# A decoder layer on Trainium2: identity transposes ahead of the first rows, a new order of row scaling and loads, and one product of the second FFN issued earlier

## The chip, the cores and the metric

The kernel runs on one core of one Trainium2 chip. The metric is the time of one execution on the device in microseconds (us), as the median of several runs; lower is better. Engines are named as in the profile: PE is TensorE (matmuls), PEld its weight loads, DVE is VectorE, ACT is ScalarE, POOL is GpSimd, and SP is SyncE, which issues most of the DMAs.

## The reference, cut to what matters

One layer works on 1,024 tokens of width 1,024, ahead of which 16 learned meta tokens stand, all in float32:

```
h = h + 1/2 * SwiGLU_1(RMSNorm(h))            # first FFN,  D_FF = 2816
u = RMSNorm(h) @ W_in
o = concat[ HGRN2(u_hgrn), StickBreaking(u_sb) ]
h = h + o @ W_out
h = h + 1/2 * SwiGLU_2(RMSNorm(h))            # second FFN
SwiGLU(h):  g, u = split(h @ w_in);  (silu(g) * u) @ w_out
RMSNorm(x): x * rsqrt(mean(x*x) + 1e-6) * gain
```

The change touches two places: the first microseconds of the first FFN (its norm, and the turning of x so that the width lies on partitions) and the first products of the second FFN's `w_in`.

## The kernel before, in words

**Products.** Each float32 operand is kept as a rounded part (hi, type float32r) and a remainder (lo), and a product is three matmuls per block of 128: hi by hi, lo by hi, hi by lo (`times`, L448). ACT makes the hi part and DVE subtracts for the lo part: for weights in `operand` (L358, the rows L360 and L362), for tokens in `first` (L834, the rows L837 and L838) or in `halve` (L304, the rows L309 and L310).

**The FFN's first matrix.** `fast_in` (L350) multiplies 2 by 2 blocks by a fast scheme with seven products: B11, B21, T2, T3, T1, T4, B22, each one of 12 matmuls (4 blocks by 3) into the PSUM banks qa, qb and qc. A `quad` is a generator that issues the products of one column; a `pair` is two quads, one for the gate and one for the up half. The first pairs are `opened`: their products are issued in an order written out by hand, a `next(...)` at a time, because the operands are still being made. In the first FFN there are four opened pairs, with the order in `open_tokens` (L792); in the second FFN there are two, and after their B11 and B21 products `in_turns` (L585) takes turns between gate and up. An opened quad of the second FFN has a step that only fetches the next weights (`ready.append(next(w))`, L498) ahead of its T2 product (L500). Before the change line 601 steps `opened[0]`, the first gate, over that fetch, and not `opened[1]`, its up half. So in the turns the gate issues T2 while the up half fetches, then the gate issues T3 and the up half T2.

**Operands of the second FFN.** B11 and B21 come from the first 512 tokens, the T operands also from the second 512 tokens. `blocks_b` (L321) makes them bit by bit: each `next(feed)` makes the next group, and T3's group (L341 to L343) is requested when the first T3 product is about to be issued (L465 and L466).

**The first rows.** `open_tokens` loads four tiles of 128 rows of x (`ra`, L840, `rows_in` at L809, 512 KB each, on SP's queue). Each row is squared and summed (`row_sum`, L759: ACT's Square with an accumulator, or a DVE operation), its root taken on ACT and inverted on DVE (`row_root`, L768), and the tile scaled on DVE (`row_scale`, L774). PE then turns 128 by 128 blocks against the identity (`turned`, L780) into PSUM, six of the eight blocks of each row tile first. `first` multiplies by the norm's gain g1 and splits. The second four tiles (`rb`, L852) are summed, scaled and turned later, in a list of items (L924 to L933) that interleaves with the opened products.

**What sets the order.** PE's order is that of the program everywhere. In `open_tokens` the orders of ACT, DVE and SP are those of the program too (L1904); elsewhere a scheduler at build time places the instructions of these engines. Instructions of one engine run in order.

**The gain.** g1 is a 4 KB vector that is spread over 128 partitions in pieces of 4 bytes. It is loaded by a DMA that ACT issues (L104), before anything else. `ng1`, its negative, is made on DVE at L1826 and is used in `combine` (L881).

Of the kernel before, what the change touches and what calls it, by code (L numbers as in the profile page):

```python
# [11 lines left out]
F32 = mybir.dt.float32  # L12
# [8 lines left out]
P = 128  # L21
D = 1024
KT = D // P
SEQ = 1024
META = 16
# [23 lines left out]
class Block:  # L49
# [19 lines left out]
    def setup(self):  # L69
        nc, a = self.nc, self.a  # L70
        self.loads = []
        self.const = c = self.pool("const")
        c.tile([P, 368], F32, name="base")
        self.pool("edge", side="right").tile([P, 504], F32, name="edge")
        self.dram = self.pool("scratch", space=DRAM)

        self.ident = c.tile([P, P], F32, name="ident")
        nc.vector.memset(self.ident, 1.0)
        nc.gpsimd.affine_select(
            out=self.ident, in_=self.ident, pattern=[[-1, P]],  # L80
            compare_op=ALU.is_equal, fill=0.0, base=0, channel_multiplier=1,
        )
        self.ones_d = c.tile([P, P], F32, name="ones_d")
        nc.vector.memset(self.ones_d, 1.0 / D)
        self.eps = c.tile([P, 1], F32, name="eps")
        nc.vector.memset(self.eps, EPS)
        nc.scalar.activation(c.tile([P, 1], F32, name="root"), self.eps, AF.Sqrt)

        self.g1 = self.column(a["ffn1_norm"][0], KT, "g1")
        self.gm = self.column(a["mix_norm"][0], KT, "gm")  # L90
        self.g2 = self.column(a["ffn2_norm"][0], KT, "g2")
        self.og = self.column(a["hgrn_out_norm"][0], 4, "og")
        self.l0 = self.column(a["hgrn_lb_logits"][0], 4, "l0")
        self.l1 = self.column(a["hgrn_lb_logits"][1], 4, "l1")
        self.qg, self.kg, self.qg8 = (c.tile([P, 1], F32, name=x) for x in ("qg", "kg", "qg8"))
        for h in range(2):
            s = slice(64 * h, 64 * h + 64)
            self.loads.append((self.qg[s], a["sb_q_norm"].rearrange("a d -> d a")))
            self.loads.append((self.kg[s], a["sb_k_norm"].rearrange("a d -> d a")))
        self.mx, self.lb, self.lbc = (c.tile([P, 4], F32, name=x) for x in ("mx", "lb", "lbc"))  # L100
        self.masks = c.tile([P, len(LEVELS), P], U8, name="masks")
        self.ss = c.tile([P, 9, 2], F32, name="ss_x")
        self.ng1 = c.tile([P, KT], F32, name="ng1")
        nc.scalar.dma_start(*self.loads.pop(0))  # L104

    def setup_rest(self):

# [242 lines left out]
    def fast_in(self, ops, n, w_in, actD, openers, ev0, open_ev, feed=None, meta=None, spare=None,  # L350
                between=lambda: None, after_opened=lambda: None, late=lambda: None, taken=lambda at, step=True: None):

        nc = self.nc
# [240 lines left out]
        opened = [q for f in range(0, 2 * openers, 2) for q in pair(f, "first")]  # L594
        if feed:
            for i in range(0, 2 * openers, 2):
                for _ in range(2):
                    for q in opened[i : i + 2]:
                        next(q)
                        yield  # L600
            next(opened[0])
            next(feed)
            made_yet.add("T2")
        else:
            yield opened, prepare
# [186 lines left out]
    def open_tokens(self, ops, opened, prepare, rows_at, ev, operands):  # L792
# [9 lines left out]
        nc, x = self.nc, self.a["x"][0]  # L802
        stt, sub = nc.vector.scalar_tensor_tensor, nc.vector.tensor_sub
        g = [self.g1[:, k : k + 1] for k in range(KT)]
        rp = self.pool("rows", ctx=rows_at, side="right")
        junk = [rp.tile([P, D], (BF16, U8)[i], name=f"junk{i}") for i in range(2)]
        order = [q for i in range(0, len(opened), 2) for _ in range(2) for q in opened[i : i + 2]]

        def rows_in(r0):  # L809
            got = []  # L810
            for i in range(4):
                row = rp.tile([P, D], F32, tag="row", name="row", bufs=8)
                nc.sync.dma_start(row, x[r0 + i * P : r0 + i * P + P])
                got.append(row)
            return got
# [14 lines left out]
        def spare(*ks):  # L830
            for k in ks:
                nc.scalar.mul((b11 + b21)[k], kept[k], g[k])

        def first(*ks):  # L834
            for k in ks:
                hi, lo = (t[:, k % 4, :] for t in ops[("B11", "B21")[k // 4]])
                nc.scalar.mul(hi, kept[k], g[k])  # L837
                stt(lo, kept[k], g[k], hi.bitcast(F32), ALU.mult, ALU.subtract)  # L838

        ra = rows_in(0)  # L840
        self.masks_blank(sd)
        for i in range(3):
            self.row_sum(ra[i], i, junk, nc.vector if i == 1 else nc.scalar)
            self.row_root(ra[i], i)
        for i in range(3):
            self.row_scale(ra[i], i)
        self.row_sum(ra[3], 3, junk, nc.scalar)
        self.row_root(ra[3], 3)
        self.row_scale(ra[3], 3, 2)
        next(order[0])  # L850
        next(order[1])
        rb = rows_in(512)  # L852
        meta = rp.tile([META, D], F32, name="meta")
        kept.update(self.turned(ra, range(6), "bbccdd"))
        first(0, 1, 2, 3)
        nc.vector.tensor_scalar_mul(b11[0], kept[0], g[0])
        spare(1)
        next(order[2])
        nc.sync.dma_start(meta, self.a["meta_tokens"])
        first(4, 5)  # L860
        self.row_sum(rb[0], 4, junk, nc.vector)
        next(order[0])
        next(order[1])
        kept.update(self.turned(ra, (6, 7), "bb"))
        first(6, 7)
        next(order[3])

        def turn_b22():
# [907 lines left out]
    def run(self):  # L1776
        nc, tc, a = self.nc, self.tc, self.a
# [20 lines left out]
        with ExitStack() as c0:  # L1798
            with ExitStack() as c1:
# [8 lines left out]
                with tc.manual_schedule(engines={nc.tensor.engine}), ExitStack() as c2:  # L1808
# [14 lines left out]
                    operands(xa, ("B11", "B21"))  # L1823
                    self.pin = self.pool("pin1", 1, PSUM, c2)
                    self.t_bufs, self.in_bufs = 2, 10
                    nc.vector.tensor_scalar_mul(self.ng1, self.g1, -1.0)  # L1826

                    def ahead_of_time(pool):

# [73 lines left out]
                    opened, prepare = next(steps)  # L1903
# [266 lines left out]
                with tc.manual_schedule(engines={nc.tensor.engine}):  # L2170
# [7 lines left out]
                    with ExitStack() as c2:  # L2178
                        self.att.append(self.pool("att1", ctx=c2))
                        tag = self.proj_tags[0]  # L2180
# [214 lines left out]
```

## Time and profile before

| | |
|---|---|
| runs | 1955.10, 1956.52, 1956.65 us; median 1956.52 |
| the profiled execution's own time | 1955.73 us |
| its span, first to last instruction | 1953.8 us |
| PE busy | 1918.7 us (98%) |
| DVE busy | 1394.1 us (71%) |
| ACT busy | 849.2 us (43%) |

The profile is one execution. Times in its views count from the start of the span. The timeline merges neighbouring instructions of one kind on one engine: start, duration of the group, engine, line, operation, output and inputs, shapes and count; in brackets stands the idle time of the engine ahead of it and what ended that. A row with SPq or ACTq is the issue of a DMA and not its transfer.

### The profile page before, as it was taken

What the parts mean: (1) busy time and instruction counts of PE and PEld (TensorE: products, weight loads), DVE (VectorE), ACT (ScalarE), POOL (GpSimd) and SP (SyncE); (2) the same over time, 40 slices, a digit from 0 to 9 for tenths busy, and PEclk for the clock granted to TensorE, in tenths of its full rate; (3) what the DMA queues carried; (4) which work ended last, traced back from release to release, by engine and by line L of the source; (5) the groups of instructions that cost most, each with busy time, mean ns of one, the idle gap of its engine ahead of it and who ended that gap; (6) DMA issues with size and microseconds to landing.
All of it is one profiled execution on the core that took longest, in us unless ns stands there. A gap on an engine that the chain in (4) does not pass through costs nothing.

```text
span 1953.8 us, 30198 instructions
## 1 busy us (share of the span) xinstructions
PE 1918.7 (98%) x10607; PEld 1616.5 (83%) x10607; DVE 1394.1 (71%) x2184; ACT 849.2 (43%) x1711; POOL 451.2 (23%) x625
## 2 busy tenths in 40 slices
PE   7999999999999999999999999999999999999999
PEld 6888888887888888888898978887888888888887
DVE  6977778877678665467777766667567767766774
ACT  6523343334444544356666635533233332344443
POOL 3010100001000003133333332210544644530000
PEclk9999999999999999999999999999999999999999
DMA  7356888757976315865453178655544444469473
GB/s 212 93 158 177 249 278 256 233 193 282 373 235 189 126 55 143 192 172 148 134 153 115 57 252 242 151 207 185 193 118 135 131 129 125 129 244 323 150 232 113
DMA packets 381687, 355.54 MB, mean 182 GB/s; under 512 B 129040, under 2 KB 284560, under 8 KB 381536
## 3 DMA queue, kind: packets, MB, share of 16 engines
q1 hardware_dynamic: 359728, 288.98, 49.0%
q0 software_dynamic: 20768, 64.63, 9.6%
q8 instruction: 84, 1.38, 0.3%
q14 instruction: 67, 0.55, 0.1%
q10 hardware_dynamic: 1040, 0.00, 0.0%
HBM read 237.95 MB, written 115.57 MB: 181 GB/s over the span
## 4 chain that ended last, share of the span: by engine, by line
PE 91%; DVE 5%; ACT 2%; issue 1%; POOL 1%; DMA 1%; SPq 0%; DVEq 0%; ACTq 0%; POOLq 0%
PE o L734 21%; PE qb L452 18%; PE qc L452 12%; PE qa L452 12%; PE proj L249 5%; PE proj L251 5%; PE proj L250 5%; PE flip L1497 2%; PE wo L249 1%; PE wo L251 1%; PE wo L250 1%; PE mq L1003 1%; PE oacc L1574 1%; PE oacc L1572 1%; PE z L1642 1%
## 5 line engine op out<-in xcount | busy, mean ns | idle before, releaser
L452 PE MATMUL qb<-T,wh 128*128 128x512 f32 x1056 | 344.6, 390 | 1.6 <-ACT T L309 0.8
L452 PEld LDWEIGHTS qb<-T,wh 128*128 128x128 f32 x1056 | 198.1, 188 | 47.0 <-issue 3.2
L452 PE MATMUL qa<-B,wh 128*128 128x512 f32 x696 | 227.7, 392 | 0.0
L362 DVE TENSOR_TENSOR wl<-s,wh 128x512 fp32r<-128x512 f32 x160 | 166.0, 1037 | 68.8 <-ACT wh L360 67.8
L249 PE MATMUL proj<-xh,wh 128*128 128x512 f32 (+2 forms) x640 | 212.4, 332 | 2.6 <-ACT st L1144 1.3
L734 PE MATMUL o<-t,w 128*128 128x512 f32 x924 | 212.1, 390 | 1.0 <-DVE u L545 0.9
L251 PE MATMUL proj<-xl,wh 128*128 128x512 f32 (+2 forms) x640 | 209.8, 328 | 0.8 <-DVE xl L1959 0.8
L250 PE MATMUL proj<-xh,wl 128*128 128x512 f32 (+2 forms) x640 | 209.7, 328 | 0.0
L734 PE MATMUL o<-parts 128*128 128x512 f32 x924 | 209.6, 389 | 0.0
L452 PE MATMUL qb<-T,wl 128*128 128x512 f32 x528 | 205.5, 389 | 0.0
L734 PEld LDWEIGHTS o<-t,w 128*128 128x128 f32 x924 | 172.7, 188 | 38.4 <-ACT sgm L983 1.2
L734 PEld LDWEIGHTS o<-parts 128*128 128x128 f32 x924 | 173.4, 188 | 36.0
L360 ACT CAST wh<-s 128x512 fp32r<-128x512 f32 x160 | 99.5, 623 | 185.2 <-PE qb L452 140.4
L452 PEld LDWEIGHTS qa<-B,wh 128*128 128x128 f32 x696 | 130.6, 188 | 28.6 <-issue 1.2
L360 ACT CAST wh<-raw 128x512 fp32r<-128x512 f32 x120 | 74.6, 622 | 144.6 <-PE qc L452 100.1
L452 PE MATMUL qa<-B,wl 128*128 128x512 f32 x348 | 135.5, 390 | 0.0
L249 PEld LDWEIGHTS proj<-xh,wh 128*128 128x128 f32 x640 | 120.4, 188 | 14.9 <-ACT st L1144 2.0
L251 PEld LDWEIGHTS proj<-xl,wh 128*128 128x128 f32 x640 | 120.4, 188 | 12.1 <-DVE xl L1959 1.2
L250 PEld LDWEIGHTS proj<-xh,wl 128*128 128x128 f32 x640 | 120.4, 188 | 9.9
L452 PE MATMUL qc<-T,wh 128*128 128x512 f32 x352 | 116.1, 391 | 0.0
L452 PEld LDWEIGHTS qb<-T,wl 128*128 128x128 f32 x528 | 99.1, 188 | 20.3
L452 PE MATMUL qc<-B,wh 128*128 128x512 f32 x352 | 114.7, 389 | 0.0
(393 smaller groups left out, 3826.8 us busy)
## 6 DMA issues: line engine op xcount, KB each, us to landing
raw<-in_ffn_w_in_dram SPq DMA_DIRECT2D x176, 256.0 KB, 4.0
raw<-in_ffn_w_out_dram SPq DMA_DIRECT2D x112, 256.0 KB, 4.5
w2in<-both SPq DMA_DIRECT2D x28, 512.0 KB, 4.1
raw<-in_w_in_dram SPq DMA_DIRECT2D x25, 512.0 KB, 5.3
ks<-kD SPq DMA_DIRECT2D x32, 260.0 KB, 4.8
wout<-both SPq DMA_DIRECT2D x16, 512.0 KB, 3.8
wh<-w2in SPq DMA_DIRECT2D x27, 256.0 KB, 3.1
wl<-w2in SPq DMA_DIRECT2D x27, 256.0 KB, 3.2
```

The lines of the kernel that those rows point to most:

```text
L249: nc.tensor.matmul(ps, wh[:, s], xs, start=k == 0, stop=False)
L250: nc.tensor.matmul(ps, wl[:, s], xs, start=False, stop=False)
L251: nc.tensor.matmul(ps, wh[:, s], xl[:, k, c0 : c0 + n], start=False, stop=k == nk - 1)
L360: nc.scalar.copy(hi, src)
L362: self.block_lo = nc.vector.tensor_sub(lo, src, hi.bitcast(F32))
L452: nc.tensor.matmul(ps, a[:, k, :], b[:, k, :], start=start and k == 0 and i == 0, stop=k == 3 and i == 2, skip_group_check=True,)
L734: nc.tensor.matmul(banks[bank][m], y[:, m * P : (m + 1) * P], z, start=start and at == 0 and e == 0, stop=q == nq - 1 and e == 2, skip_gro ...
L1003: nc.tensor.matmul(ps[at : at + 32, :], self.xm[:, 4 * h + k, :], got[i, h][:, k, :], start=h == 0 and k == 0, stop=h == 1 and k == 3, til ...
L1497: self.nc.tensor.transpose(ps[:m, j, :], src[:, s0 : s0 + m], self.ident)
L1572: nc.tensor.matmul(o[:, c], vj, w[0], start=j == 0, stop=False, skip_group_check=True)
L1574: nc.tensor.matmul(o[:64, c], vj[:, :64], w[1], start=False, stop=end, skip_group_check=True)
L1642: nc.tensor.matmul(z, q, ks[0][:, s0 : s0 + n], start=True, stop=False)
```

## The change

In the first rows:

- The load of g1 leaves ACT's queue; SP issues it, behind the four loads of `ra`.
- Thirty transposes of the identity by itself go to PE ahead of the rows. They write two PSUM tiles of the tag qb that nothing reads.
- The sum of row tile 1 moves from DVE to ACT, that of tile 2 from ACT to DVE. Tiles 0 and 1 are scaled directly behind their own roots, tile 2 behind these; before, the three were scaled after all three roots.
- The first weight block of the first up half (`next(order[1])`) is loaded and split behind the first four blocks of `first`, not ahead of the transposes. The second weight block of the gate (`order[2]`) stays behind it, the loads of `rb` follow both, and the second block of the up half follows blocks 6 and 7.
- The sum of `rb[0]` moves behind blocks 6 and 7, and `ng1` is made behind that.

In the second FFN: `opened[1]` is stepped over its fetch too, so that the turns begin with the gate's T2, the up half's T2, the gate's T3, the up half's T3.

```diff
@@ setup
-        nc.scalar.dma_start(*self.loads.pop(0))
@@ fast_in
             next(opened[0])
+            next(opened[1])
             next(feed)
             made_yet.add("T2")
@@ open_tokens
         ra = rows_in(0)
+        nc.sync.dma_start(*self.loads.pop(0))
+        for _ in range(2):
+            warm = self.pin.tile([P, 512], F32, tag="qb", name="warm", bufs=2)
+            for i in range(15):
+                t = warm[:, P * (i % 4) : P * (i % 4) + P]
+                nc.tensor.transpose(t, self.ident, self.ident)
         self.masks_blank(sd)
-        for i in range(3):
-            self.row_sum(ra[i], i, junk, nc.vector if i == 1 else nc.scalar)
+        for i in range(2):
+            self.row_sum(ra[i], i, junk, nc.scalar)
+            if i == 1:
+                self.row_sum(ra[2], 2, junk, nc.vector)
             self.row_root(ra[i], i)
-        for i in range(3):
             self.row_scale(ra[i], i)
+        self.row_root(ra[2], 2)
+        self.row_scale(ra[2], 2)
         self.row_sum(ra[3], 3, junk, nc.scalar)
         self.row_root(ra[3], 3)
         self.row_scale(ra[3], 3, 2)
         next(order[0])
-        next(order[1])
-        rb = rows_in(512)
-        meta = rp.tile([META, D], F32, name="meta")
         kept.update(self.turned(ra, range(6), "bbccdd"))
         first(0, 1, 2, 3)
         nc.vector.tensor_scalar_mul(b11[0], kept[0], g[0])
         spare(1)
+        next(order[1])
         next(order[2])
+        rb = rows_in(512)
+        meta = rp.tile([META, D], F32, name="meta")
         nc.sync.dma_start(meta, self.a["meta_tokens"])
         first(4, 5)
-        self.row_sum(rb[0], 4, junk, nc.vector)
         next(order[0])
-        next(order[1])
         kept.update(self.turned(ra, (6, 7), "bb"))
         first(6, 7)
+        next(order[1])
+        self.row_sum(rb[0], 4, junk, nc.vector)
+        nc.vector.tensor_scalar_mul(self.ng1, self.g1, -1.0)
         next(order[3])
@@ run
-                    nc.vector.tensor_scalar_mul(self.ng1, self.g1, -1.0)
```

## The prediction

> **What bounds the kernel now.** I read the page first, then the timeline of the first 30 us, that of the second FFN's opening, and last some stretches of the DMA and the clock.
>
> ```profile
> PE 1918.7 (98%) x10607; PEld 1616.5 (83%) x10607; DVE 1394.1 (71%) x2184; ACT 849.2 (43%) x1711; POOL 451.2 (23%) x625
> PE   7999999999999999999999999999999999999999
> ```
>
> PE is busy in 1918.7 of 1953.8 us. So a change that leaves the matmuls alone can win only where PE is idle, or runs slowly: in the first slice of 49 us, and in short waits. The timeline of the first slice:
>
> ```profile
> 1.79 0.29 POOL L79 TENSOR_SCALAR_AFFINE_SELECT ident<-ident 128x128 f32<-128x128 f32 x1
> 7.11 1.23 DVE L763 SCALAR_TENSOR_TENSOR junk<-row 128x1024 uint8<-128x1024 f32 x1 [0.85 <-DMA row<-in_x_dram]
> 8.38 0.30 ACT L771 ACTIVATE ss_x<-ss_x,eps 128x1 f32<-128x1 f32 x1 [2.32 <-DVE junk L763]
> 8.58 1.04 ACT L766 ACTIVATE junk<-row 128x1024 bf16<-128x1024 f32 x1
> 9.94 1.04 ACT L766 ACTIVATE junk<-row 128x1024 bf16<-128x1024 f32 x1
> 10.16 2.08 DVE L778 TENSOR_SCALAR row<-row,ss_x 128x1024 f32<-128x1024 f32 x3
> 11.06 5.35 PE L787 MATMUL xps<-ident,row 128*128 128x128 f32 x24 [11.06 <-POOL sd L129]
> 11.11 0.29 ACT L771 ACTIVATE ss_x<-ss_x,eps 128x1 f32<-128x1 f32 x1
> 12.15 0.15 DVE L772 RECIPROCAL ss_x<-ss_x 128x1 f32<-128x1 f32 x1
> 12.35 0.88 DVE L778 TENSOR_SCALAR row<-row,ss_x 128x512 f32<-128x512 f32 x2
> 13.14 1.36 DVE L362 TENSOR_TENSOR wl<-raw,wh 128x512 fp32r<-128x512 f32 x2
> 15.38 2.43 ACT L837 ACTIVATE B<-xps,g 128x512 fp32r<-128x512 f32 x4 [2.94 <-PE xps L787]
> 16.10 2.73 DVE L838 SCALAR_TENSOR_TENSOR B<-xps,g,B 128x512 fp32r<-128x512 f32 x4 [1.59 <-ACT B L837]
> 16.12 0.80 PE L452 MATMUL qa<-B,wh 128*128 128x512 f32 x1
> 16.71 0.48 PE L452 MATMUL qa<-B,wl 128*128 128x512 f32 x1
> 17.71 0.61 PE L452 MATMUL qa<-B,wh 128*128 128x512 f32 x2
> 19.30 1.22 PE L787 MATMUL xps<-ident,row 128*128 128x128 f32 x8
> 20.28 0.48 PE L452 MATMUL qa<-B,wh 128*128 128x512 f32 x1
> ```
>
> PE's first instruction is at 11.06, its first product at 16.12. The idle 11.06 us are put down to POOL's masks, which `turned` does not read: the identity stood at 2.08 (1.79 + 0.29), and PE waited for the first scaled row (from 10.16, first of three, 0.69 each, done by 10.9). The 24 transposes then run at 5.35 / 24 = 0.22 us each and hold ACT for 2.94 us, although row 3 was scaled by 13.23 (12.35 + 0.88). The eight at 19.30 take only 1.22 / 8 = 0.15, tail included: PE was at half its clock before. The first matmuls say the same: 16.12 to 16.71 is 0.59 from start to start, later ones in a group of two (17.71, 0.61 long) stand about 0.23 apart.
>
> **The first rows, step by step.** T is the time at which DVE starts the first lo part: 16.10 before. Everything behind T is paced by DVE (2.73 / 4 = 0.68 per block) and PE.
>
> When rows land: row 1 at 7.1 (DVE's wait at 7.11 ends on it). The DMA in half microseconds, and its queues from 3 to 5.5:
>
> ```profile
> 3.50:4.00 0.50, 0.00 (x0) 0.00 (x0) 0.00 (x0) 0.00 (x0) 0.50 (x2) 1.00 0.84 231
> 4.00:4.50 0.50, 0.00 (x0) 0.00 (x0) 0.00 (x0) 0.00 (x0) 0.50 (x2) 1.00 0.95 71
> 4.50:5.00 0.50, 0.00 (x0) 0.00 (x0) 0.00 (x0) 0.42 (x1) 0.50 (x2) 1.00 0.86 239
> 6.00:6.50 0.50, 0.00 (x0) 0.00 (x0) 0.16 (x1) 0.06 (x1) 0.50 (x2) 1.00 1.04 418
> q10 hardware_dynamic: 1040, 0.00, 23.0%
> 0.80 0.46 ACTq L104 DMA_DIRECT2D g<-in_ffn_norm_dram  x1
> 5.76 0.22 DVE L1826 TENSOR_SCALAR ng<-g 128x8 f32<-128x8 f32 x1 [3.60 <-DMA g<-in_ffn_norm_dram]
> ```
>
> The first four rows are of the stretches; the last two numbers of each are the DMA's busy share and GB/s. At 418 GB/s a row of 512 KB takes 1.25 us, so row 2 lands at about 8.4 and row 3 at 9.6. Between 3.5 and 5 the engines are busy and move little: g1's 1,040 packets (q10) hold them. They cost the rows 23% of 2.5 us = 0.58 us by the queue's share, and ((418-231) + (418-71) + (418-239)) x 0.5 / 418 = 0.85 us by the missing bytes. Behind the rows this is theirs again: row 2 lands at 7.55 to 7.8.
>
> The new chain, with row 2 landing at L: DVE sums it in 1.27 (7.11 to the root at 8.38), inverts the root of row 1 (0.18), scales row 1 (0.69), inverts and scales row 2 (0.19 + 0.69): L + 3.0. On ACT the root of row 2, the sum and the root of row 3 take 0.2 + 1.17 (9.94 to 11.11) + 0.3, done at L + 2.95. So the scaling of row 3 starts at L + 3.25, DVE is free at L + 4.1, makes wl in 0.65 (half of 13.14's pair; the second moves behind the first four lo parts) and is ready for the first lo at L + 4.75. PE turns row 3 from L + 3.75 on; at the faster 0.15 the first block is there at L + 4.0, and ACT's hi (0.69) at L + 4.7. Both paths agree: T = L + 4.75. With L = 8.4 as before this gives 13.15, a gain of 2.95; with L = 7.55 to 7.8 it gives 12.3 to 12.55, a gain of 3.55 to 3.8. I take **3.5 us**.
>
> What hides the rest: the 30 transposes last 30 x 0.22 = 6.6 us at most, from 2.1 to 8.7; row 1 can't be turned before L + 2.2, about 9.9, so row 0's turn fits between, and nothing waits for them. The next weights' split (0.65) and `ng1` (0.22) now stand in DVE's queue behind T. In front of the up half's product, which PE reaches at T + 4.2 (20.28 stood to 16.10 like that), DVE has 0.68 x 4 + 0.66 + 0.65, done at T + 4.0. The 0.9 us more in that queue end in the idle time that DVE has next:
>
> ```profile
> 28.03 0.69 DVE L362 TENSOR_TENSOR wl<-raw,wh 128x512 fp32r<-128x512 f32 x1 [1.75 <-ACT wh L360]
> ```
>
> `rb` and meta pass behind one more load of 256 KB (0.6 us at 418 GB/s): behind g1 and three such loads `rb[0]` lands near 13. Its sum stands behind all eight lo parts, at T + 8 x 0.68 + 0.66 + 3 x 0.65 = T + 8, past 20, so it is hidden; without that cover DVE would stall for what is missing. The load of g1 passes behind the rows on SP. ACT needs it at L + 4.0, about 11.8. Alone on the DMA it would take 0.6 to 0.85 us behind row 3 (9.0), so it is there by 10.5 or so; from its issue on ACT to the end of DVE's wait for it took 5.76 - 0.80 = 5.0 us beside the rows. If the row order costs it 2 us more, T moves by under 1 us.
>
> **The clock.** This needs PE to be fast by about 12. Three stretches of 3.41 us and less:
>
> ```profile
> 1948.84:1952.25 3.41, 0.86 (x4) 0.38 (x2) 1.59 (x3) 0.00 (x0) 0.00 (x0) 1.00 0.80 308
> 1952.26:1953.70 1.44, 0.00 (x0) 0.00 (x0) 0.00 (x0) 0.00 (x0) 0.00 (x0) 0.50 0.00 0
> 1217.50:1220.91 3.41, 1.91 (x11) 1.25 (x9) 3.41 (x6) 0.67 (x2) 0.87 (x1) 1.00 1.03 357
> ```
>
> The column ahead of the DMA share is the granted clock. At the end PE was busy for 0.86 of 3.41 us, and then the clock was 0.50; in the thinnest stretch inside, with 1.91 of 3.41, it stayed at 1.00. Behind the warming-up PE turns three rows by 6 x 0.15 each and has about half of its time filled, near the second case: I expect the clock to hold. That transposes raise it at all is read from the first timeline: they were nearly all that PE had done when the matmuls at 16.7 sped up. The Trainium skill says otherwise ("TensorE: Matmul & The Clock Gate", Part 4: PE-mode transpose): transposes don't count as work for the clock gate. By that rule the products would still start cold. The rows above speak against it, but I keep it as a rival.
>
> **The second FFN.**
>
> ```profile
> 1338.92 0.39 PE L452 MATMUL qb<-T,wh 128*128 128x512 f32 x1
> 1341.42 0.39 PE L452 MATMUL qb<-T,wh 128*128 128x512 f32 x1
> 1341.84 0.69 DVE L484 TENSOR_TENSOR u<-qb,p 128x512 f32<-128x512 f32 x1
> 1342.63 0.47 PE L452 MATMUL qb<-T,wh 128*128 128x512 f32 x1 [0.83 <-ACT T L309]
> 1343.65 0.69 DVE L342 TENSOR_TENSOR hT<-hT 128x512 f32<-128x512 f32 x1
> 1344.25 2.49 DVE L310 TENSOR_TENSOR T<-hT,T 128x512 fp32r<-128x512 f32 x4
> 1344.37 0.62 ACT L309 CAST T<-hT 128x512 fp32r<-128x512 f32 x1 [1.88 <-DVE hT L342]
> 1346.20 0.73 PE L452 MATMUL qb<-T,wh 128*128 128x512 f32 x2 [0.42 <-DVE T L310]
> 1349.05 0.39 PE L452 MATMUL qb<-T,wh 128*128 128x512 f32 x1
> ```
>
> The gate's T2 starts its 12 matmuls from 1338.92 to 1341.42, 2.50 us. Its T3 starts 1.0 us late, at 1342.63 for 1341.65, and takes 3.57 to its last one at 1346.20: the delay is 1.0 + 1.07 = 2.1 us. With the up half's T2, long ready, in between, T3 starts at 1344.37 and needs its last lo, which was there by 1346.20, for its last matmul at 1344.37 + 2.50 = 1346.87. That leaves 0.67 us: room for one more DVE step of 0.60, the up half's own sum (L484), which now comes among T3's steps. Best, all 2.1 us go. At worst this sum stands ahead of two lo parts, the last difference, its cast and its lo: it can't start before 1344.5, and 0.6 + 1.2 + 0.7 + 0.75 + 0.7 later, at about 1348.4, T3's last matmul starts, where before the later of T3 and up T2 started its last matmul at 1349.05: 0.6 us gained. I take **2.0 us**, since the gate's sum at 1341.84 stood just where its product ended and not ahead of ready work. The weights of the up half are fetched one product earlier, which nothing waits for.
>
> **Sum.** 3.5 + 2.0 = 5.5 us. Against the profiled execution's own 1955.73 that is 1950.2; this execution is 0.8 below the median shown, 1956.52, from which it gives 1951.0. About 0.2%, 3.9 us, is what a measurement here can tell from no change. Behind both places PE is packed and its neighbours are released by it, so I carry the sum to the end whole.
>
> **Rivals.**
>
> 1. The clock isn't up when the products start, since transposes don't raise it or since the thin stretch before 12 drops it again. The matmuls then start some 0.45 apart instead of 0.23 for one or two stretches of 3.4 us: half of that is lost, 1.7 to 3.4. Gain 5.5 - 2.6 = 2.9, **1953.6**. For it: 0.86 of 3.41 was too little at the end. Against it: 16.7 came 5.6 us after the first transpose. Chance 0.12.
> 2. One gain is used up further on: up T2's sum stands ahead of T3's steps (0.6 instead of 2.0), or a stage behind the first rows is paced by a load and takes the 3.5 back. Gain 2 to 4, about **1953.5**. For it: DVE is busy for 71%. Against it: its idle 1.75 us at 28.03 is longer than the 0.9 added. Chance 0.12.
> 3. Slower: g1 comes late. ACT's first block, and all products behind it, wait for its 1,024 pieces, which are now last but for the weights in SP's queue. It decides from a landing at 11.8 + 5.5 = 17.3 on; if it took thrice the 5.0 us from row 3's landing on, it would land at 9 + 15 = 24, and 24 - 17.3 = 6.7 would be lost, **1963**; at twice, 19, it is 1.7 and **1958**, within 0.2%. Against it: the 0.58 to 0.85 us of DMA time above. Chance 0.04, and 0.02 for other losses.
>
> That the change doesn't do what it says would need the warming-up to start late; POOL's identity at 2.08 speaks against that.
>
> **How the numbers follow.** My forecast, 1951.0, has 0.70. Its own range: 2.95 + 0.6 = 3.5 to 3.8 + 2.1 = 5.9 gained, and half a microsecond for the runs' own scatter: 1950.0 to 1953.0. The 8-in-10 range takes in most of rivals 1 and 2: 1949.4 to 1954.2. Faster by over 0.2% is below 1952.6: nearly all of the forecast and a part of the first two rivals, 0.76. Same 0.18, slower 0.06.
>
> **What would show it.** In the changed profile: 30 matmuls `warm` on PE from 2.1 to below 9; rows turned in four groups; the last row's six at 0.15 or less; the first `qa` product between 12.3 and 13.2, with matmuls 0.23 apart from the start; DVE's lo steps behind it without a wait for g1; T3 of the second FFN without a gap, 24 T2 matmuls ahead of it. I'm wrong if the first product starts after 14, if its matmuls are 0.45 apart, if T3 still waits over 0.5 us, or if the gaps have gone and the span hasn't followed.

## The result and the profile after

| | before | changed |
|---|---|---|
| median of the runs, first series | 1955.45 us (11 runs) | 1951.12 us (11 runs, 1950.41 to 1953.05) |
| ratio, 95% interval | | 0.9977, 0.9970 to 0.9985 |
| median of a second series | 1955.49 us (23 runs) | 1952.29 us (11 runs, 1950.04 to 1954.31) |
| ratio, 95% interval | | 0.9984, 0.9975 to 0.9993 |
| profiled execution: time, span | 1955.73, 1953.8 | 1950.51, 1948.7 |

The forecast was 1951.0. The ratios stand for 4.5 us (2.9 to 5.9) and 3.1 us (1.4 to 4.9). In the last series two executions of other kernels, of 2452.46 and 6830.71 us, were disturbed and are left out of every median and ratio here.

The page of the changed kernel, busy time and PE by slices:

```profile
PE 1922.2 (99%) x10637; PEld 1619.9 (83%) x10637; DVE 1392.9 (71%) x2184; ACT 848.4 (44%) x1711; POOL 449.1 (23%) x625
PE   9999999999999999999999999999999999999999
```

PE has the 30 new matmuls (10,637 for 10,607), and the 7 of the first slice has gone. The timeline of the first rows:

```profile
2.13 6.18 PE L846 MATMUL warm<-ident 128*128 128x128 f32 x30 [2.13 <-POOL ident L79]
2.67 0.49 SPq L841 DMA_DIRECT2D g<-in_ffn_norm_dram  x1
7.78 1.23 DVE L763 SCALAR_TENSOR_TENSOR junk<-row 128x1024 uint8<-128x1024 f32 x1 [0.66 <-DMA row<-in_x_dram]
8.15 0.99 PE L787 MATMUL xps<-ident,row 128*128 128x128 f32 x6
10.00 2.44 PE L787 MATMUL xps<-ident,row 128*128 128x128 f32 x18 [0.86 <-DVE row L778]
10.95 0.92 DVE L778 TENSOR_SCALAR row<-row,ss_x 128x512 f32<-128x512 f32 x2
11.79 0.72 DVE L361 TENSOR_TENSOR wl<-raw,wh 128x512 fp32r<-128x512 f32 x1
11.92 2.42 ACT L837 ACTIVATE B<-xps,g 128x512 fp32r<-128x512 f32 x4 [0.70 <-PE xps L787]
12.64 2.73 DVE L838 SCALAR_TENSOR_TENSOR B<-xps,g,B 128x512 fp32r<-128x512 f32 x4
12.66 0.50 PE L451 MATMUL qa<-B,wh 128*128 128x512 f32 x1 [0.23 <-ACT B L837]
13.00 0.40 PE L451 MATMUL qa<-B,wl 128*128 128x512 f32 x1
```

Row 2 is there at 7.75 (DVE's wait at 7.78 ends on it), and DVE starts the first lo part at T = 12.64, 4.89 us later; before it was 16.10. g1, issued on SP at 2.67, delays nobody: its landing is recorded at 9.40, and ACT's first block at 11.92 waited for PE. The first product starts 3.46 us earlier, and its second matmul 0.34 behind the first, where it was 0.59. The second FFN:

```profile
1336.08 0.39 PE L451 MATMUL qb<-T,wh 128*128 128x512 f32 x1
1341.53 0.62 ACT L308 CAST T<-hT 128x512 fp32r<-128x512 f32 x1 [1.88 <-DVE hT L341]
1341.97 0.62 PE L451 MATMUL qb<-T,wh 128*128 128x512 f32 x2
1342.01 0.68 DVE L483 TENSOR_TENSOR u<-qb,p 128x512 f32<-128x512 f32 x1
1342.61 1.88 DVE L309 TENSOR_TENSOR T<-hT,T 128x512 fp32r<-128x512 f32 x3
```

The 24 T2 matmuls run from 1336.08 on, T3 follows at once at about 1341.5, and no PE row there has a wait in brackets any more. The up half's sum (1342.01) does stand ahead of the last lo parts, but these still come in time. From the gate's T2 (1338.92 before, 1336.08 now, 2.85 earlier) to the end of the turns the lead grows to 5.05 us: 2.2 us here. It is also the lead at the end of the span, so of 3.46 at the start 2.85 arrived at the second FFN. (Lead is how much earlier the same matmul, counted without the warming-up, starts than in the kernel before.) The second profile of the same kernel shows how little of that is sure: 3.16 us were won at T (12.94), nothing of it was left at the gate's T2 (a lead of -0.01), and the same 2.2 us came there.

### The profile page after: what moved, and what is told of

Read it like the earlier page. It is cut to its first block, busy times and chain, and to the rows that moved or that the text cites. A ratio compares the mean times of both kernels' runs of the same rounds, so it can differ in the third digit from the quotient of the medians.

```text
span 1948.7 us, 30258 instructions
## 1 busy us (share of the span) xinstructions
PE 1922.2 (99%) x10637; PEld 1619.9 (83%) x10637; DVE 1392.9 (71%) x2184; ACT 848.4 (44%) x1711; POOL 449.1 (23%) x625
## 4 chain that ended last, share of the span: by engine, by line
PE 82%; issue 6%; DVE 5%; DMA 2%; ACT 2%; POOL 1%; SPq 1%; DVEq 0%; POOLq 0%; ACTq 0%
PE o L734 21%; PE qb L451 15%; PE qa L451 12%; PE qc L451 10%; PE proj L248 4%; PE proj L250 4%; PE proj L249 4%; PE flip L1507 2%; PE wo L248 1%; PE wo L249 1%; PE wo L250 1%; PE oacc L1584 1%; PE oacc L1582 1%; DVE KB L1269 1%; PE z L1652 1%
```

## The experiments

Theory: the time follows from the two gains, 3.5 us at T and 2.0 in the second FFN, carried to the end; the 30 transposes are needed, since they raise the clock ahead of the row turns. Rivals: one of the parts is used up further on; the transposes do nothing. Behind the first series there are three more, on three chips (e1 to e4; e5 to e8; the second runs, e9 and e10), each with its own runs of the kernel before (medians 1955.27, 1955.99, 1955.49). A difference to the kernel before is worked out from the ratio, which is not the quotient of the medians; one between two other kernels is that of their medians, with the interval from resampled runs. The changed kernel's own two series lie 1.2 us apart (0.6 to 2.5), so kernels are best compared within a series. L is the landing of row 2. "Wait" is the time that PE loses ahead of its matmul number 1220 (warming-up not counted), a product of the first FFN near 217 us; it is spoken of below. "Below 1" counts the runs whose mean granted clock was under 1.000.

| kernel | median us | ratio, 95% interval | T | T - L | wait | below 1 |
|---|---|---|---|---|---|---|
| before | 1955.5 | 1 | 16.10 | 7.7 | 0 | 19 of 89 |
| changed | 1951.12 | 0.9977 (0.9970 to 0.9985) | 12.64 | 4.89 | 0.58 | 7 of 11 |
| the same, again | 1952.29 | 0.9984 (0.9975 to 0.9993) | 12.94 | 4.94 | 1.56 | 9 of 11 |
| e1 front only | 1952.69 | 0.9989 (0.9980 to 0.9998) | 12.83 | 4.90 | 1.55 | 6 of 11 |
| e2 second FFN only | 1953.42 | 0.9992 (0.9983 to 1.0001) | 16.07 | 7.7 | 0 | 4 of 11 |
| e3 no transposes | 1950.40 | 0.9975 (0.9965 to 0.9984) | 13.95 | 6.04 | 0 | 1 of 9 |
| e3 again | 1950.11 | 0.9975 (0.9965 to 0.9986) | 13.28 | 5.97 | 0 | 1 of 7 |
| e4 transposes only | 1957.70 | 1.0011 (1.0002 to 1.0019) | 14.90 | 6.7 | 0.50 | 11 of 11 |
| e5 g1 on ACT | 1954.20 | 0.9988 (0.9979 to 0.9996) | 13.22 | 4.86 | 0.82 | 10 of 12 |
| e6 60 transposes | 1952.99 | 0.9985 (0.9977 to 0.9994) | 14.84 | 7.7 | 0 | 8 of 10 |
| e7 old row order | 1953.99 | 0.9989 (0.9980 to 0.9997) | 13.14 | 6.14 | 1.05 | 7 of 12 |
| e8 second split ahead | 1952.06 | 0.9977 (0.9968 to 0.9985) | 12.31 | 5.39 | 0.73 | 6 of 12 |
| e9 gap filled | 1950.06 | 0.9972 (0.9961 to 0.9984) | 12.64 | 4.94 | 0 | 4 of 6 |
| e10 no transposes, second split ahead | 1950.46 | 0.9973 (0.9963 to 0.9983) | 13.01 | 6.00 | 0 | 2 of 8 |

### e1 and e2: each part alone

e1 is the changed kernel without its line in `fast_in`:

```diff
             next(opened[0])
-            next(opened[1])
             next(feed)
```

> The changed kernel with the second FFN's opening as it was (the up half isn't stepped over its fetch). My theory: the two gains add and don't touch each other. The first lo part starts at 12.6 us as in the changed kernel, 3.4 to 3.5 us earlier than before; the gate's T3 in the second FFN waits for its operands again, 2.1 us in all. Time 3 us below the kernel before (2.2 us above the changed kernel, about 1953 against 1951.1). Rival, that a gain at the start is used up on the way and the whole result comes from the second FFN: the second FFN's first T2 product starts less than 1 us earlier than before, and the time is within 1 us of the kernel before.

e2 is the kernel before with that line:

```diff
             next(opened[0])
+            next(opened[1])
             next(feed)
```

> The kernel before with only the second FFN's step. My theory: nothing differs up to the second FFN; there T3 has no gap and the time falls by 2.0 to 2.2 us (1955.4 to about 1953.3). Rival, that the up half's sum stands ahead of T3's steps on VectorE when the start is not shifted: T3 still waits for 1.5 us and the time falls by 0.6.

Measured: 2.2 us (0.4 to 3.9) for the front, 1.6 us (-0.2 to 3.3) for the second FFN. In e1 PE waits there as before:

```profile
1343.67 0.47 PE L451 MATMUL qb<-T,wh 128*128 128x512 f32 x1 [0.83 <-ACT T L308]
1347.23 0.73 PE L451 MATMUL qb<-T,wh 128*128 128x512 f32 x2 [0.42 <-DVE T L309]
```

In e2 neither wait is there, while the front stays where it was. So the two parts act where they were said to act, each without the other, and together they come to 3.8 us, beside the 3.1 and 4.5 us measured for both. The second FFN's part isn't clear of zero in e2's runs, but all profiles agree on it: from the gate's T2 to the end of the turns the lead grows by 2.2 us in each of the eleven profiles with the new line, and by nothing in the two without it (e1 and e4). The front's part is less sure: in e1's profiled execution, its slowest, a lead of 3.27 us at T had turned into -1.03 at the gate's T2.

### e3 and its second run: without the 30 transposes

```diff
-        for _ in range(2):
-            warm = self.pin.tile([P, 512], F32, tag="qb", name="warm", bufs=2)
...
-                nc.tensor.transpose(t, self.ident, self.ident)
```

> The changed kernel without the 30 identity transposes. My theory, that transposes raise the clock: row 0 is turned from about 6.7 us at 0.21 us a transpose, the rows follow each other at that speed, row 3's first block is there at about 13 and the first lo part starts at 13.5 to 13.9 (1 us later); the first matmuls stand 0.43 apart until a stretch of 3.4 us was full, at 15 to 17 us, which costs 0.5 to 1.5 more. Time 1.5 to 2.5 us above the changed kernel. Rival, that transposes don't count as work: the clock rises at the same moment with and without them, and the time is that of the changed kernel within 0.5 us.

The expected loss at T is there, that of the time isn't. The timeline of PE in e3:

```profile
7.27 1.51 PE L787 MATMUL xps<-ident,row 128*128 128x128 f32 x6 [7.27 <-DVE row L778]
10.15 3.66 PE L787 MATMUL xps<-ident,row 128*128 128x128 f32 x18 [1.37 <-DVE ss_x L772]
13.97 0.50 PE L451 MATMUL qa<-B,wh 128*128 128x512 f32 x1 [0.16 <-ACT B L837]
14.31 0.40 PE L451 MATMUL qa<-B,wl 128*128 128x512 f32 x1
```

The 18 turns take 3.66 us instead of 2.44, T stands 6.0 us behind row 2 instead of 4.9, and yet the products run at full speed from the first: 0.34 to the second matmul, as in the changed kernel. Row turns alone had raised the clock (at 13.21). In the three profiles without transposes it rises 0.15 to 0.8 us ahead of the first product, so not with much to spare. The time is no worse than that of the changed kernel. This was repeated beside it in the last series.

> The changed kernel itself, a second time, beside three others on the same chip: ratio to the kernel before 0.9977 as the first time (-4.5 us). In its profile the first lo part starts some 4.9 us behind the landing of row 2 and the first lateness of TensorE behind it is the wait for the sum u at product 1220 (near 217 us), because the SP load of the block in front of it lands near 212.8 us whatever the front does. Theory A (the 30 transposes are worth nothing at the end, since that load takes back what they give): the same time as the kernel without them, within 0.7 us. Theory B (they are worth the 1.3 us that the first products start earlier): 1.3 us below that kernel. Theory C (they do harm, since an early clock meets more thin windows): 0.7 us or more above it.

> Leaves out only the 30 turns of the identity, a second time, now in one series with the changed kernel. First lo part near 13.9 us, 6.0 us behind row 2's landing. Theory A: the time of the changed kernel within 0.7 us, and the wait at product 1220 is shorter by about what the start is later (0 to 0.1 us instead of 0.6). Theory B: 1.3 us above it. Theory C: 0.7 us or more below it.

The kernel without transposes is 2.2 us faster than the changed one (1950.11 for 1952.29; 0.5 to 3.8); over both series 1.4 us (0.2 to 2.5; 16 and 22 runs). The transposes give 1.1 us at T, and it isn't kept: theory B falls. C has the sign; A's reason, the wait at 1220, is in the table, but holds only a part. More is lost near 860 us (see below). Runs of full clock differ by less: 1950.7 for the six of the changed kernel, 1950.0 and 1950.1 in the two series without transposes.

### e4 and e6: the transposes alone, and twice as many

e4 puts the 30 transposes into the kernel before, at the same place:

```diff
         ra = rows_in(0)
+        for _ in range(2):
+            warm = self.pin.tile([P, 512], F32, tag="qb", name="warm", bufs=2)
+            for i in range(15):
+                t = warm[:, P * (i % 4) : P * (i % 4) + P]
+                nc.tensor.transpose(t, self.ident, self.ident)
         self.masks_blank(sd)
```

> The kernel before with only the 30 identity transposes. My theory: transposes of the rows take 0.11 us each instead of 0.21 and are done at about 13.5; what is late next is VectorE, which scales all rows in one block and then splits two weight blocks, until 14.5. The first lo part starts at 14.5 instead of 16.1, and the time falls by 1.6 us (1955.4 to 1953.9). Rival, that the speed of PE alone makes the gain at the start: the first lo part starts at 13.7 or earlier and the time falls by 2.4 us or more. Second rival, that transposes don't raise the clock: no gain.

It is slower than before, by 2.2 us (0.4 to 3.7). Its timeline of PE, and then the stretch in front of the drop of the clock and the drop itself:

```profile
2.13 5.04 PE L845 MATMUL warm<-ident 128*128 128x128 f32 x30 [2.13 <-POOL ident L79]
10.97 4.24 PE L787 MATMUL xps<-ident,row 128*128 128x128 f32 x24 [3.80 <-DVE row L778]
14.92 0.79 PE L452 MATMUL qa<-B,wh 128*128 128x512 f32 x1
```

```profile
8.74:12.16 3.42, 1.19 (x11) 1.22 (x12) 2.22 (x6) 3.36 (x8) 3.42 (x10) 1.00 1.10 400
12.16:15.57 3.41, 3.41 (x17) 3.15 (x15) 2.89 (x6) 1.57 (x4) 2.35 (x6) 0.50 1.03 403
```

The rows are scaled late in the old order, PE is idle for 3.80 us, and behind a stretch with 1.19 of 3.42 us of work the clock falls to half until 15.57, when the turns and the first products run: rival 1 in its second form. The first lo part starts at 14.90 and not at 14.5. This isn't what makes e4 slower than before, though: before, the clock was low until 16.90, and T is still 1.20 us earlier here. The lead is lost later. Past product 1220 it is 0.59 us; past a second wait for a sum, ahead of product 1513, it is -0.24:

```profile
274.31 0.47 PE L452 MATMUL qb<-T,wh 128*128 128x512 f32 x1 [1.04 <-DVE u L484]
```

Ahead of a second clock drop near 865 us it is -0.10, and past it -2.20. So in both row orders (before and e4, e3 and the changed kernel) the transposes bring T forward by 1.1 to 1.2 us and cost time at the end.

e6 doubles them:

```diff
-            for i in range(15):
+            for i in range(30):
```

> The changed kernel with 60 identity transposes instead of 30. My theory, that their cost is nothing only as long as row 0 and row 1 wait for their roots anyway: 26 at 0.21 us and 34 at 0.11 end at 11.4; 24 transposes of rows at 0.11 follow without a gap, row 3's first block is there at 13.5 instead of 11.9, and the first lo part starts at 14.1 to 14.3, 1.5 us later; time 1.5 us above the changed kernel. Rival, that TensorE is not on the path at all here: T and time as in the changed kernel.

They end at 11.84 and hold the row turns back; T is 2.2 us later than in the changed kernel. T - L is 2.85 us longer, most of the 30 x 0.11 = 3.3 us that were added: with the cover gone, a transpose costs nearly its own length at T. At the end this isn't shown. In its own series e6 is 0.9 us slower than e8 (-0.7 to 2.6), and its profiled execution, without a wait at 1220 and without a clock drop, is as short as the changed kernel's first (1949.0 and 1948.7).

### e5, e7 and e8: the order of the front

e5 lets ACT issue g1 as before:

```diff
+        nc.scalar.dma_start(*self.loads.pop(0))
...
         ra = rows_in(0)
-        nc.sync.dma_start(*self.loads.pop(0))
```

> The changed kernel with g1 loaded on ScalarE's queue again, ahead of the rows. My theory: its 1,024 pieces of 4 bytes hold the DMA engines again, rows 2 and 3 land 0.6 us later (VectorE's sum of row 2 starts at 8.4 instead of 7.8), and the first lo part starts at 13.2 instead of 12.6; time 0.6 us above the changed kernel. Rival, that g1's place is of no weight (the rows land as before since they were limited by the start of their own queue): the sum of row 2 starts at 7.8 as in the changed kernel, and the time is the same. Second rival, that a late g1 holds ScalarE in the changed kernel: the first block of hi parts starts earlier here.

e7 has the old order of the row sums and scalings in the changed kernel:

```diff
-        for i in range(2):
-            self.row_sum(ra[i], i, junk, nc.scalar)
-            if i == 1:
-                self.row_sum(ra[2], 2, junk, nc.vector)
+        for i in range(3):
+            self.row_sum(ra[i], i, junk, nc.vector if i == 1 else nc.scalar)
             self.row_root(ra[i], i)
+        for i in range(3):
             self.row_scale(ra[i], i)
-        self.row_root(ra[2], 2)
-        self.row_scale(ra[2], 2)
```

> The changed kernel with the old order of the rows' sums and scales (row 1 summed on VectorE, rows 0 and 2 on ScalarE, all three scaled behind the three roots). My theory: the sum of row 2 on ScalarE ends at about 9.0, its root at 9.3, and VectorE scales three rows from 9.4 to 11.5; row 3 is scaled from 11.7 instead of 10.95. The first lo part starts at 13.3 to 13.4, 0.7 us later; time 0.7 us above the changed kernel. Rival, that the order is of no weight since row 3's landing decides: T within 0.2 us of the changed kernel's.

e8 takes the second block's split ahead of the four blocks again:

```diff
         next(order[0])
+        next(order[1])
         kept.update(self.turned(ra, range(6), "bbccdd"))
...
         spare(1)
-        next(order[1])
```

> The changed kernel with the up half's first weight block split ahead of the transposes again. My theory: VectorE splits two blocks in a row behind the scaling of row 3, and the first lo part starts 0.65 us later, at 13.3; what was behind T is then shorter by as much, but the products of the first four blocks are paced by the lo parts, so all products shift by 0.6 us; time 0.6 us above the changed kernel. Rival, that the second split only changes its place in the same queue and the total stays: the second product (of the up half) starts at the same time as in the changed kernel, 16.8, and the time is the same.

g1: row 2 lands between 8.25 and 8.37 in the four kernels with g1 on ACT, between 6.92 and 8.00 (mean 7.46) in the ten with g1 on SP: 0.87 us earlier, with a scatter of 1.1. In e5's series row 2 lands at 8.36 with g1 on ACT and at 6.92 to 7.10 in the other three; in that of e1 to e4 at 8.25 and 8.35 against 7.91 and 7.93. So the direction is sure and the size, 0.3 to 1.4 us, is not. In e5 nothing else at T differs (T - L = 4.86). The row order is worth 1.25 us of T - L (6.14 in e7), as e7's rows are all scaled behind the last root, and PE has no row until 10.12. The place of the second split: T - L is 0.5 us longer in e8. The up half's first product starts at 16.48 and not 16.82, but only because row 2 landed 0.83 us earlier in this profile; it stands 4.17 us behind T as in the changed kernel (4.18), so behind row 2 it is 0.5 us late too, as the theory said. That half microsecond isn't seen in the time: the ratio is that of the changed kernel. e5 and e7 are slower than e8 by 2.1 (0.5 to 3.4) and 1.9 us (0.7 to 3.1), which is more than their T says. In e7's profile 2.1 us of the lead go between 1154 and 1187 us, where PE waits 2.1 us for the transfer of a tile `oT`; in the kernel before it doesn't wait for it.

### e9 and e10: two versions that keep more

e9 adds eight turns of the identity between the turns of row 0 and row 1 (the 0.86 us of PE's wait at 10.00):

```diff
         for i, row in enumerate(rows):
+            if fill and i == 1:
+                idle = self.pin.tile([P, 512], F32, tag="qa", name="warm", bufs=2)
+                for j in range(fill):
+                    t = idle[:, P * (j % 4) : P * (j % 4) + P]
+                    nc.tensor.transpose(t, self.ident, self.ident)
```

> The changed kernel with 8 more turns of the identity between the turn of row 0 and that of row 1, where TensorE waits 0.86 us: 8 of 0.109 us fill it. If the clock is lost in some executions between the first transposes and the products, this window is the one that loses it, and the time falls by 0.5 us or more below the changed kernel, with fewer runs whose mean clock is under 1.0. If the drops lie elsewhere (near 860 us, as four profiles showed), the time stays within 0.5 us of it. First lo part 4.9 to 5.1 us behind row 2 either way.

e10 is e3 with e8's order.

> Without the 30 turns, and the second block's split taken ahead of the first four turned tiles. If the front's time from the first lo part to the second block's product sets the end, it gains what that order gained at the up product before (0.3 to 0.5 us) on the kernel without the turns; if the load in front of product 1220 or the waits at 1160 to 1221 us take such gains back, it is the same within 0.7 us. First lo part 6.0 to 6.5 us behind row 2.

e9 is 2.2 us faster than the changed kernel beside it (0.8 to 3.8; against both series of it 1.6, 0.0 to 2.6), though T is the same to 0.05 us behind row 2, and though its clock isn't better kept: 4 of 6 runs are below 1, and its profile has a drop at 860.9. So the expected reason fails, and the difference must come from behind T. The profiles name one place, in the first FFN near 200 us. In the changed kernel, the timeline of DVE and PE:

```profile
201.16 0.69 DVE L534 TENSOR_TENSOR sg<-qb,p 128x512 f32<-128x512 f32 x1 [1.87 <-DMA act13T<-sg]
212.85 0.69 DVE L381 TENSOR_TENSOR s<-raw 128x512 f32<-128x512 f32 x1 [0.60 <-DMA raw<-in_ffn_w_in_dram]
215.99 0.68 DVE L483 TENSOR_TENSOR u<-qb,p 128x512 f32<-128x512 f32 x1
216.82 0.47 PE L451 MATMUL qb<-T,wh 128*128 128x512 f32 x1 [0.42 <-DVE u L483]
```

Read from the end: PE waits for the sum u, DVE was held up by a weight load, and this load was issued late on SP because DVE had waited for the store `act13T` to leave its tile. In e9 DVE starts the same instruction without that wait, 1.9 us earlier, and no wait of PE follows:

```profile
199.27 0.68 DVE L534 TENSOR_TENSOR sg<-qb,p 128x512 f32<-128x512 f32 x1
```

The store was issued at 196.44 and 196.51 in the two kernels and took 4.60 and 2.60 us to land. The DMA's queues from 196.4 to 201.1, first of the changed kernel, then of e9:

```profile
q0 software_dynamic: 233, 0.76, 40.7%
q1 hardware_dynamic: 1054, 0.13, 16.3%
q8 instruction: 1, 0.02, 1.6%
```

```profile
q0 software_dynamic: 240, 0.79, 41.6%
q1 hardware_dynamic: 1056, 0.13, 16.2%
```

One packet of 16,384 bytes, a block of instructions, lies in the first and not in the second. By the trace's packet records it runs from 198.51 for 1.17 us; the store's packets are through by 198.7, all but the last few, which end at 200.1 and 200.5, behind the block. In e9 a block comes at 190.0. Over the 14 profiles the store takes 2.6 to 3.05 us in six (e2, e3 twice, e6, e9, e10), and PE never waits at 1220 in them. It takes 4.4 to 5.1 us in eight, with a wait of 0.5 to 1.6 us in all but the kernel before, where the load lands 199.4 us behind T and DVE is still busy; in the changed kernel's two profiles it lands 200.1 and 201.1 behind T. In all eight a block starts 1.7 to 2.7 us behind the store's issue. In e6 and e9 none is near; in the other four of the six it starts 2.4 to 2.5 us behind the issue, when the store is nearly through. That e5 and e7, at 2.7 and 2.6, are among the late ones doesn't fit so simple a reading. Both kernels that were profiled twice fell twice in the same group. So the time of the fetch seems to belong to the compiled kernel, and instructions put ahead of everything move it. The block was not moved by itself: its price, 0.6 and 1.6 us in the changed kernel's two profiles, is inferred and not shown.

e10 has T - L = 6.0, no wait, and the time of e3. The medians of e3, e9 and e10 lie within 0.4 us of each other, and each is below that of the changed kernel beside it (e10 by 1.8 us, 0.2 to 3.3).

### The clock near 860 us

In six of the nine profiles of kernels with 30 transposes or more, but in none of the five without them, the granted clock falls to half for one stretch of 3.41 us, in one of them two, in the weave of the stick-breaking products. The changed kernel's second profile, and the same stretches of its first:

```profile
860.08:863.49 3.41, 2.03 (x8) 1.01 (x7) 3.14 (x6) 3.01 (x9) 1.29 (x4) 1.00 0.65 187
863.49:866.90 3.41, 3.40 (x10) 2.80 (x10) 3.20 (x4) 2.10 (x6) 1.89 (x2) 0.50 1.03 210
```

```profile
860.08:863.49 3.41, 2.18 (x9) 1.32 (x10) 3.14 (x5) 3.01 (x9) 1.29 (x4) 1.00 0.76 214
863.49:866.90 3.41, 3.41 (x18) 2.77 (x16) 3.19 (x6) 1.70 (x7) 1.94 (x3) 1.00 1.01 204
```

Ten matmuls for 18: its lag behind the first profile grows by 1.55 us there, from 0.36 to 1.91. Half of 3.41 us in 1950 is 0.0009 of a mean clock, so a run at 0.999 has lost about one such stretch; up to 2 us at half clock behind the last products count too, and make 0.9995 by themselves in e3's second profile. In the two series of the changed kernel such runs are 16 of 22, median 1952.1, against 1950.7 for the six at 1.000; without transposes they are 4 of 24.

The clock changes on a grid that begins with its first rise (6.74 in the second profile, 251 x 3.413 us ahead of the drop at 863.49), so these stretches lie on the second profile's grid and not on the first's. On its own grid the first profile has

```profile
857.62:861.03 3.41, 2.42 (x10) 1.21 (x8) 3.09 (x7) 3.22 (x11) 0.00 (x0) 1.00 0.45 149
861.03:864.44 3.41, 2.54 (x12) 1.85 (x13) 3.30 (x4) 3.01 (x10) 1.72 (x5) 1.00 0.87 214
```

Its thin place is cut in two. In the six profiles with a drop the stretch of the grid ahead of it holds 1.98 to 2.29 us of PE's work; in the eight others every stretch between 855 and 868 us holds 2.42 or more. And the place itself is thinner in all nine kernels with transposes (1.97 to 2.16 us in its thinnest 3.41, wherever the grid lies) than in the five without (2.43 or 2.44). So by these profiles a drop takes a thin place and a grid that doesn't divide it.

In all nine, and in none of the five, PE waits there once more, for 0.39 to 0.64 us ahead of matmul 4939. It waits for ACT, and ACT had waited for a weight load. In the changed kernel and in e3:

```profile
856.59 1.05 ACT L231 CAST wh<-raw 128x1024 fp32r<-128x1024 f32 x1 [2.44 <-DMA raw<-in_w_in_dram]
```

```profile
855.88 1.05 ACT L231 CAST wh<-raw 128x1024 fp32r<-128x1024 f32 x1 [2.30 <-DMA raw<-in_w_in_dram]
```

PE's matmul 4920 starts at 855.70 and 856.48 in them. So the load lands 0.9 us behind that matmul in the first and 0.6 ahead of it in the second; over the profiles 0.1 to 0.9 behind in the nine, 0.5 to 0.6 ahead in the five. Here too a block of instructions stands beside the load: it starts within 0.3 us of matmul 4920 in the five, 4.7 to 5.3 us ahead of it in the eight with 30 or 38 transposes, and 9.8 us ahead in e6 with 60. So the block's place against the program moves with the number of instructions ahead of it. That it makes the load late is inferred, and e6, where no block is near and the load is late too, doesn't fit. The cost is measured: from matmul 4930 to 4965 the lead falls by 0.0 us in the other four without transposes, by 0.6 to 0.9 in the three of the nine without a drop, by 1.5 to 2.2 with one and by 3.4 with two. In the changed kernel's two profiles this and the wait at 1220 come to 1.5 and 3.8 us, more than the 1.1 us that the transposes give.

## Why the prediction was right

**The clock and the transposes.** In the changed profile PE's spacing falls from 0.213 to 0.109 us at 7.69, among the identity's own turns, and the clock holds through the gap at 9.1 to 10.0. In e3 row turns alone raise it. By the Trainium skill's rule ("TensorE: Matmul & The Clock Gate", Part 4: PE-mode transpose), which doesn't count transposes as work, both should have been cold; the trace disagrees. So rival 1 fails for this kernel in its first form; its second form, a thin stretch ahead of the products, comes true only in e4's row order. (The prediction's stretch of 1.91 in 3.41 us, the thinnest that it found, didn't lie on the grid of that execution; on it the thinnest holds 1.84, and kept the clock too.) Wrong was the silent step from there: that what the transposes give is in the time. Their 1.1 us at T is measured, and their removal costs nothing at the end.

**The front.** L + 4.75 was forecast and L + 4.89 measured (4.86 to 4.94 in four other profiles of kernels that keep this order of rows). g1's move was to bring row 2 by 0.58 to 0.85 us forward; 0.62 in the profile, 0.87 over the 14. T moved by 3.46 for 3.5.

**The second FFN.** 2.2 us for 2.0, in every profile with the new line; the up half's sum came among the T3 steps without a price.

**Carried to the end whole.** This is the step that was too generous. 3.46 + 2.2 = 5.7 us were won locally, 5.05 arrived in the first profile and 2.06 in the second, and the ratios say 4.5 and 3.1 us. Behind T PE is packed, but packed against a lead that loads and stores allow: the first 0.55 us went at product 1220 (1.6 in the second profile), and near 860 us another 0.9 went, or 2.2 with the clock drop that most runs seem to have. That is rival 2's "a stage is paced by a load", in a small form.

**Luck in the number.** The first series' median fell within 0.2 us of the forecast, and over all 22 runs it is 1951.6. But the forecast took 5.5 us off 1956.52, the median of three runs; the eleven runs that these three belong to gave 1955.45. The base was 1.1 us too high and the gain 1.0 too large, and these two cancelled. The range leans the same way: with half a microsecond for scatter its upper end is 1956.5 - 3.5 + 0.5 = 1953.5 and not 1953.0.

**Rival 3** needed g1 after 17.3; it landed at 9.40.

## What to carry to other kernels

A gain at the start is worth its length only as far as the loads behind it leave room; look for the transfers whose landing stood just ahead of their reader, and follow the lead of the same instruction through the trace. Judge warming-up by the end and not by the first product: 30 transposes brought it forward by 1.1 to 1.2 us in both row orders, and both kernels were slower at the end than without them. Where the real work warms the engine in time they can be left out. Judge an edit of one or two microseconds by runs and by several profiles, since added instructions also move the blocks in which code is fetched.

## What was not expected of the hardware

- Instruction blocks of 16,384 bytes (84 packets in the changed execution) share the DMA with the data, 0.9 to 1.7 us each where they were looked at; a store with one close behind it took 4.4 to 5.1 us in eight profiles, and 2.6 to 3.05 in the others. Near 860 us a block starts about 5 us earlier, against the matmul beside it, in the kernels with 30 transposes at the start than in those without, and 10 us earlier in the one with 60.
- The granted clock changes at multiples of 3.41 us, counted from the first rise in each execution, and falls for a whole stretch in the middle of a kernel that is 99% busy. The share of work that decides isn't clear from these runs: 1.19 of 3.42 us lost it, and so did 2.29 of 3.41 in e9 near 860 us, while the stretch from 6.74 to 10.15 in the changed kernel's second profile, with 1.94, kept it, and so did one with 2.00 from 215.01.
- Landings of row 2 scatter by 1.1 us over the ten profiles with the same order of row loads (6.92 to 8.00), and by 0.6 us between two profiles of one kernel (e3).
